# Delta rule with the heads in pairs: one generator for two heads, one inversion row for 64 blocks, shared buffer slots

## Chip, cores and metric

One core of one Trainium2 chip runs the whole program in one launch. The metric is the device time of the program in microseconds (us). The kernel before takes 1430.65 us, the median of 3 runs (1429.36 to 1430.66). Everything is fp32 at the program's edges; the large products are taken as sums of three products of "fp32r" halves (hi·hi, hi·lo, lo·hi).

## What is computed

One step of a decoder layer for a prompt of 1024 tokens and 8 samples of one token each, so 1032 columns in all. The normalised input is multiplied by one wide matrix `w_in`. Its columns feed a short gated convolution (branch A) and a gated DeltaNet with 8 heads of 128 by 128 (branch B); both are projected, gated, merged and projected again. What matters here is the delta rule of branch B, which runs in chunks (128 tokens in the kernel, so 8 chunks). In the reference, for one head and one chunk:

```python
decay = exp(where(causal, gc[:, None] - gc[None, :], -inf))
a_mat = where(strict, (kb @ k.T) * decay, 0) + eye(C)
u, w  = split(triangular_solve(a_mat, [v * beta, kb * exp(gc)]))
attn  = (q @ k.T) * decay
# scan over the chunks, state S (128 x 128):
v_new = u - w @ S
o     = (q * exp(gc)) @ S + attn @ v_new
S     = S * exp(gc_last) + (k * exp(gc_last - gc)).T @ v_new
```

q and k are l2-normalised, `gc` is the running sum of the log decay, and o then goes through an RMSNorm and a gate silu(zB). The 8 samples take one step each of the same recurrence from a given state, per head.

## The kernel before

Python generates a fixed instruction stream for the five engines. There are three stretches.

1. **Start** (`startup`): loads, norms, and the first product.
2. **Jobs** (`run`, line 708). A job is one 128-column slice of `w_in` against all 1032 columns of the input: 3 groups of 344 columns, 8 k-steps, 3 matmuls a step, so 72 matmuls. There are 48: per head a k, a q and a v job (`qkv_job`, line 829, whose evacuation copies PSUM to `raw` and whose follow-up generator does the 4-tap convolution and silu), 8 zB jobs (`zb_job`, line 1138) and 16 gate jobs (`gate_job`, line 1155, whose result is stored to DRAM). Each job's weights are loaded to `wraw` (`w_load`, line 688), and split into `whi` by ScalarE and `wlo` by VectorE (`w_split`, line 696) during the job before.
3. **Products** (`products`, `products_b`), then the output projections. These start from `to_products` (line 1700), which is hooked ahead of the third job from the end: it drains all generators, frees their buffers and starts to prepare operands.

Beside the jobs run generators ("strands"), one for each piece of side work: decays, delta rule, samples, convolutions. After every k-step of a job, `slot()` (line 602) resumes each strand whose own clock is due by the model in class `Sched` (line 62), which charges every instruction a cost and 450 ns of slack after each plain `yield`. So the order of the work on each engine follows a planner's costs, and a strand's TensorE work is put as a burst into a job, about between two of its k-steps.

For each head h there is a strand `decay_gen` (line 858: builds the 8 decay blocks DB and DA from a broadcast row of gc) and a strand `delta_gen` (line 886), which starts once v is there. Its steps, in order: transposes of k and q with squared sums (ScalarE) and kd (VectorE); rsqrt; the k·k and q·k products into DB and DA; the **row inversion** (line 984), 31 steps of two dependent VectorE instructions that invert all 32 by 32 diagonal blocks of the head's 8 chunks at once, 32 blocks on 128 partitions by 8 rows each, fetched through DRAM (sA, At before; sT, Tn after); then TensorE joins the 32-blocks to 64 and 128 ("inversion bursts" of 32 by 32 and 64 by 64 matmuls; lines 1015 to 1046); then the recurrence over 8 chunks, three bursts a chunk: k·S and q·S; U·X; kd·vn and DA·vn. VectorE makes X and S between them, ScalarE copies vn. Last, the norm, transposes and the product with sz, and a store to yBsc. Flags hold the heads in order: the inversion's result may enter U only when the head before is done (line 1006), and the buffers of head h wait for head h-2.

The sample work of head h is `sample_gen` (line 1231). It waits for the flag "qs", which `delta_gen` sets at its very beginning, and for the samples of the head before.

Buffers: `T4` is a set of 6 equal slots (class `Slots`, line 635) that are lent and given back; the strands' large tiles (U, DB, DA, kd, vp, kq) have buffers of their own, by two or three. `wraw` has two. The order of the jobs (lines 1383 to 1394) is k, q, v, one gate, then zB of the head before; eight more gates close it, with the last zB as the third of them.

On the DMA side, nearly all transfers are issued by SyncE, one queue in program order.

Of the kernel before, what the change touches and what calls it, by code (L numbers as in the profile page):

```python
# [16 lines left out]
P = 128  # L17
# [18 lines left out]
NT4 = 6  # L36
# [3 lines left out]
NSL, NSR = 22, 7  # L40
# [5 lines left out]
FILL = (1, 1, 1, 1, 1, 1, 1, 1)  # L46
# [15 lines left out]
class Sched:  # L62


    def __init__(self):
        self.clk = dict.fromkeys(("V", "A", "PE", "GP", "SY", "DMA"), 0.0)
        self.cur = None
        self.chain = True
        self.table = None
        self.cold, self.run = True, 0.0  # L70

    def note(self, eng, cost, lat=0.0):
# [42 lines left out]
class Paced:  # L115
# [3 lines left out]
    def __getattr__(self, op):  # L119
# [3 lines left out]
        def call(*args, **kw):  # L123
# [7 lines left out]
            elif n == "PE":  # L131
                if op == "transpose":
                    s.note(n, max(size, out.shape[0]) * 2 / 2.4 + 2.0)
                elif kw["rhs"].dtype == F32:
                    s.note(n, 4 * max(size, kw["lhsT"].shape[-1]) / 2.4 + 4.0)
# [22 lines left out]
def hybrid_step(  # L158
# [110 lines left out]
    gsc = dram.tile([NC * NH, C], F32, name="gsc")  # L269
# [9 lines left out]
    rsc = dram.tile([NH, NB, P], F32, name="rsc")  # L279

# [407 lines left out]
    def w_load(jobs, i):  # L688
# [3 lines left out]
        raw = wpool.tile([P, NK, P], F32, tag="wraw", name="wraw", bufs=2)  # L692
# [16 lines left out]
    def run(jobs, first, stop):  # L709
        for i in range(first, stop):  # L710
# [3 lines left out]
            if i + 2 < stop:  # L714
                w_load(jobs, i + 2)
            _, hi, lo = wq.pop(i)
            rh, rl = src()
            for gi, (g0, gn) in enumerate(GROUPS):
# [3 lines left out]
                for k in range(NK):  # L722
# [24 lines left out]
    def ba_gen():  # L747
        ap_ = bp
        ban = ap_.tile([P, 9, 16], F32, name="ban")
# [16 lines left out]
        xg = ap_.tile([P, 9, NH], F32, name="xg")  # L766
        u = ap_.tile([P, 9, NH], F32, name="u")
        sq = ap_.tile([P, 9, NH], F32, name="sq")
        pl = ap_.tile([P, 9, NH], F32, name="pl")
# [9 lines left out]
        for n in (17, 15, 13, 11, 9, 7, 5, 3):  # L779
# [22 lines left out]
        gcr = ap_.tile([64, C], F32, name="gcr")  # L802
        V.tensor_copy(out=gcr, in_=pt[:64, 0:C])
        SY.dma_start(out=gsc, in_=gcr)
# [4 lines left out]
                     in_=smp.rearrange("a b h -> (a b h)").unsqueeze(0).to_broadcast([P, 2 * NB * NH]))  # L809
        flags["ba"] = True  # L810
# [48 lines left out]
    def decay_gen(h, st):  # L859
        while not flags.get("ba") or (h and not flags.get(("qd", h - 1))) \  # L860
                or (h > 1 and not flags.get(("inv", h - 2))):
            yield
        gcB = bp.tile([P, NC, C], F32, tag="gcB", name="gcB")
        SY.dma_start(out=gcB, in_=gsc.rearrange("(c h) i -> h c i", h=NH)[h].unsqueeze(0).to_broadcast([P, NC, C]))
        yield
        while h > 1 and not flags.get(("done", h - 2)):
            yield
        DB = bp.tile([P, NC, C], F32, tag="DB", name="DB", bufs=2)
        DA = bp.tile([P, NC, C], F32, tag="DA", name="DA", bufs=2)
        for c in range(NC):  # L870
            act(DA[:, c, :], gcB[:, c, :], AF.Identity, bias=neg["gc"][:, c, h:h + 1])
            if c % 4 == 3:
                yield
        wide = lambda m: m.unsqueeze(1).to_broadcast([P, NC, C])
        tt(DB, DA, wide(m_strict), ALU.max)
        yield
        tt(DA, DA, wide(m_causal), ALU.min)
        yield
        act(DB, DB, AF.Exp, scale=-1.0)
        act(DA, DA, AF.Exp)  # L880
        act(gcB, gcB, AF.Exp)
        st.update(gcB=gcB, DB=DB, DA=DA)

    junk = lambda: bp.tile([P, C], F32, tag="junk", name="junk", bufs=1)

    def delta_gen(h, st):
        ch = lambda a: a[:, :, h:h + 1]
        while "DA" not in st or "v" not in st or (h > 1 and not flags.get(("done", h - 2))):
            yield
        kq, vT, gcB, DB, DA = st["kq"], st["v"], st["gcB"], st["DB"], st["DA"]  # L890
        V.tensor_copy(out=qs_s[:, h, :, 0], in_=smpl(kq[:, 0, :]))
        V.tensor_copy(out=qs_s[:, h, :, 1], in_=smpl(kq[:, 1, :]))
        V.tensor_copy(out=v_s[:, h, :], in_=smpl(vT))
        flags[("qs", h)] = True


        kd = bp.tile([P, NC, C], F32, tag="kd", name="kd", bufs=2)
        ssk = bp.tile([P, NC], F32, tag="ssk", name="ssk", bufs=2)
        ssq = bp.tile([P, NC], F32, tag="ssq", name="ssq", bufs=3)
        for src, sq in ((0, ssk), (1, ssq)):  # L900
            for half in range(2):
                pt = ps_aux()
                for i in range(4):
                    c = half * 4 + i
                    transpose(pt[:, i * C:(i + 1) * C], kq[:, src, c * C:(c + 1) * C])
                sched.loose()
                for i in range(4):
                    c = half * 4 + i
                    act(junk(), pt[:, i * C:(i + 1) * C], AF.Square, accum_out=sq[:, c:c + 1])
                if src == 0:  # L910
                    tt(kd[:, half * 4:half * 4 + 4, :], pt.rearrange("p (c d) -> p c d", d=C),
                       ch(ekd)[:, half * 4:half * 4 + 4, :].to_broadcast([P, 4, C]), ALU.mult)
# [4 lines left out]
        ts(ssk, ssk, EPS, op0=ALU.add)  # L917
        rk = rsqrt(bp, ssk, P, NC, "rk")
        cB = bp.tile([P, NC], F32, tag="cB", name="cB", bufs=2)
# [1010 lines left out]
```

## Time and profile before

The profiled execution took 1428.2 us, of which 1426.1 us lie between the first and the last instruction.

| stretch, us from the span's start | what runs | matmul busy, us | weight load busy, us | VectorE busy, us | ScalarE busy, us |
|---|---|---|---|---|---|
| 58 to 817 | jobs 1 to 47 and the delta rule | 748.64 | 718.28 | 520.03 | 432.07 |
| 817 to 1202 | products | 383.61 | 382.71 | 299.69 | 135.11 |
| 1202 to 1426 | end of the products, output projections | 215.57 | 190.88 | 129.37 | 65.95 |

A profile's matmul row counts overlapping, pipelined matmuls, and their ends are modelled; the weight loads (PEld) have a row of their own. An fp32 matmul shows as two matmul records, an fp32r one as one. The granted TensorE clock is 1.00 nearly everywhere in the span.

### The profile page before, as it was taken

To read this page: it belongs to the slowest core of one execution; us is meant where nothing else is said; L and a number is where in the kernel's file an instruction comes from. 1 tells how busy PE (TensorE), PEld (TensorE's weight loads), DVE (VectorE), ACT (ScalarE), POOL (GpSimd) and SP (SyncE) were. 2 spreads that over 40 slices of the span, in tenths; PEclk is the share of its full clock that TensorE was granted. 3 is DMA by queue.
4 is the path that set the end of the run, shared out by engine and by line. 5 is a ranking of instruction groups with operands and counts; after the bars stand their busy time and mean duration, and the time that the engine had idled before them with its cause. 6 is when DMAs were issued, how large, how long until landed. Compare 5 with 4: busy or idle time off the path is not lost.

```text
span 1426.1 us, 26358 instructions
## 1 busy us (share of the span) xinstructions
PE 1394.4 (98%) x10274; PEld 1328.4 (93%) x10274; DVE 990.5 (69%) x2516; ACT 674.7 (47%) x1534; POOL 31.0 (2%) x72
## 2 busy tenths in 40 slices
PE   6999999999999999999999999999999999999997
PEld 4899998999989899998999999999999999999786
DVE  6766875697758768676463988877777787854553
ACT  6756744856466555747433433333333345432211
POOL 0000000000000000000000000000000110000000
PEclk9999999999999999999899999999999999999999
DMA  9622432153412423241332465432211876752321
GB/s 321 145 48 78 118 97 72 33 125 82 108 55 70 121 51 104 68 108 56 96 104 73 133 224 178 134 90 75 61 54 59 231 225 213 239 161 86 96 85 60
DMA packets 191591, 161.80 MB, mean 113 GB/s; under 512 B 34503, under 2 KB 167008, under 8 KB 191458
## 3 DMA queue, kind: packets, MB, share of 16 engines
q1 hardware_dynamic: 186912, 151.58, 36.0%
q0 software_dynamic: 4352, 8.46, 2.1%
q8 instruction: 81, 1.33, 0.4%
q14 instruction: 44, 0.36, 0.1%
q10 hardware_dynamic: 202, 0.08, 0.0%
HBM read 123.40 MB, written 36.91 MB: 112 GB/s over the span
## 4 chain that ended last, share of the span: by engine, by line
PE 78%; DVE 10%; DMA 6%; ACT 3%; issue 2%; SPq 1%; DVEq 0%; ACTq 0%
PE pm_t L124 53%; PE pa_t L124 23%; PE pb L124 2%; DVE wlo L124 1%; DVE Ttmp L124 1%; DVE Tw L124 1%; DMA At<-sA 1%; DVE acc L124 1%; SPq L124 1%; DMA xs<-in_x_prompt_dram 1%; DMA gcB<-gsc 1%; DVE on L124 1%; DVE mrg L124 1%; DVE vT L124 1%; DVE ro_a L124 0%
## 5 line engine op out<-in xcount | busy, mean ns | idle before, releaser
L124 PE MATMUL pm_t<-xh,whi 128*128 128x344 f32 (+1 forms) x1384 | 453.4, 328 | 0.0
L124 PE MATMUL pm_t<-xl,whi 128*128 128x344 f32 (+1 forms) x1384 | 436.2, 315 | 0.0
L124 PE MATMUL pm_t<-xh,wlo 128*128 128x344 f32 (+1 forms) x1384 | 435.8, 315 | 0.0
L124 PEld LDWEIGHTS pm_t<-xh,whi 128*128 128x128 f32 x1384 | 261.6, 189 | 1.6
L124 PEld LDWEIGHTS pm_t<-xl,whi 128*128 128x128 f32 x1384 | 261.8, 189 | 0.4
L124 PEld LDWEIGHTS pm_t<-xh,wlo 128*128 128x128 f32 x1384 | 261.2, 189 | 0.4
L124 ACT CAST whi<-wr 128x1024 fp32r<-128x1024 f32 x60 | 62.8, 1047 | 139.4 <-PE pm_t L124 65.7
L124 DVE TENSOR_TENSOR wlo<-wraw,whi 128x512 fp32r<-128x512 f32 x112 | 76.5, 688 | 35.6 <-ACT whi L124 35.1
L124 ACT CAST whi<-wraw 128x512 fp32r<-128x512 f32 x112 | 68.7, 624 | 55.8 <-PE pm_t L124 53.0
L124 PE MATMUL pm_t<-thi,wlo 128*128 128x258 f32 x304 | 86.3, 284 | 1.3 <-DVE wlo L124 1.2
L124 PE MATMUL pa_t<-thi,wlo 128*128 128x258 f32 x304 | 86.2, 284 | 0.1
L124 PE MATMUL pm_t<-tlo,whi 128*128 128x258 f32 x304 | 85.9, 283 | 0.0
L124 PE MATMUL pa_t<-tlo,whi 128*128 128x258 f32 x304 | 85.9, 283 | 0.0
L124 PE MATMUL pm_t<-thi,whi 128*128 128x258 f32 x304 | 85.8, 282 | 0.0
L124 PE MATMUL pa_t<-thi,whi 128*128 128x258 f32 x304 | 85.8, 282 | 0.0
L124 DVE TENSOR_TENSOR wlo<-wr,whi 128x1024 fp32r<-128x1024 f32 x60 | 73.2, 1220 | 10.3 <-ACT whi L124 10.1
L124 PE MATMUL pa_t<-xh,whi 128*128 128x258 f32 x256 | 72.4, 283 | 0.0
L124 PE MATMUL pa_t<-xh,wlo 128*128 128x258 f32 x256 | 72.2, 282 | 0.0
L124 PE MATMUL pa_t<-xl,whi 128*128 128x258 f32 x256 | 72.2, 282 | 0.0
L124 DVE SCALAR_TENSOR_TENSOR kq<-raw,vecs,kq 128x528 f32<-128x528 f32 x96 | 69.6, 761 | 2.4 <-ACT kq L124 2.4
L124 PE MATMUL pm_t<-ylo,whi 128*128 128x344 f32 x192 | 61.4, 321 | 0.6 <-DVE ylo L124 0.6
L124 PE MATMUL pm_t<-yhi,whi 128*128 128x344 f32 x192 | 61.4, 321 | 0.0
(397 smaller groups left out, 3065.5 us busy)
## 6 DMA issues: line engine op xcount, KB each, us to landing
wraw<-in_w_in_dram SPq DMA_DIRECT2D x48, 512.0 KB
wr<-in_w_in_dram SPq DMA_DIRECT2D x64, 256.0 KB
aw<-in_ada_w_dram SPq DMA_DIRECT2D x16, 512.0 KB
gBsc<-gate SPq DMA_DIRECT2D x8, 516.0 KB
gAsc<-gate SPq DMA_DIRECT2D x8, 516.0 KB
txs<-phi SPq DMA_DIRECT2D x8, 516.0 KB
txs<-plo SPq DMA_DIRECT2D x8, 516.0 KB
yAsc<-acc SPq DMA_DIRECT2D x8, 516.0 KB
```

The source lines that it names most:

```text
L124: r = f(*args, **kw)
```

## The change

- `delta_gen(p)` and `decay_gen(p)` serve a **pair** of heads, p = 0 to 3. Every TensorE burst holds the matmuls of both heads; small tiles (ssk, cB, nx, vs) have a head axis; VectorE's X and S steps are two instructions in a row, ScalarE's vn copy is one of twice the width.
- The **row inversion** is one for 64 blocks: 16 rows on each partition instead of 8, still 31 steps of two instructions. The 32-block joins take 4 bursts for a pair.
- The delta strand starts after the pair's last q job; v is asked for only after the inversion, and the "qs" flag, on which the samples wait, is set there. kd is parked in DRAM (kdsc) and fetched back. The decay exp(gc) of q comes as a row of its own from DRAM; DA and DB are each built from gc (four broadcast loads a pair).
- **Slots**: T4 has 16 slots of 1032 columns; U, T11, kd, DA, DB, sz, and later wlo and wsum live there. `wraw` has one buffer, and the next load is issued after the split that frees it.
- **Job order**: k q k q v v g g for pair 0; k q, zB of the pair before twice, k q v v g g for pairs 1 and 2; the last pair has four gates and its own two zB jobs; six gates close.
- **Planner**: a cost for TensorE's change between fp32 and fp32r work; the 4 us pause in `sample_gen` is gone.

Core of the diff:

```diff
-NT4 = 6
+WRAW = 1
+NT4 = 16
 DYN = 2048
 HT = NT // 2
 PW = HT // 2
-NSL, NSR = 22, 7
+NSL, NSR = 14, 7
 SAME = 115.0
 CROSS = 60.0
 LATER = {"PE": 200.0, "V": 135.0, "A": 155.0}
 SLK = 450.0
 SG = 0
-FILL = (1, 1, 1, 1, 1, 1, 1, 1)
+ORDER = (
+    "k0 q0 k1 q1 v0 v1 g g",
+    "k0 q0 y0 y1 k1 q1 v0 v1 g g",
+    "k0 q0 y0 y1 k1 q1 v0 v1 g g",
+    "k0 q0 y0 y1 k1 q1 v0 v1 g g g g z0 z1",
+)
...
+        if eng == "PE" and wide != self.wide:
+            cost += 85.0 if self.wide else 20.0
+            self.wide = wide
...
             if before:
                 before()
-            if i + 2 < stop:
-                w_load(jobs, i + 2)
...
                     if gi == 1 and k in (1, 4) and i + 1 < stop:
                         w_split(jobs, i + 1, k == 4)
+                        if k == 4 and i + 2 < stop:
+                            w_load(jobs, i + 2)
...
+        def decays(dst, i, mask, op, scale):
+            while not T4.ready(2):
+                yield
+            g_ = T4.get("gcB", S)
+            gcB = g_.rearrange("p (c i) -> p c i", i=C)
+            SY.dma_start(out=gcB, in_=gsc[0].rearrange("(c h) i -> h c i", h=NH)[h0 + i].unsqueeze(0)
+                         .to_broadcast([P, NC, C]))
+            yield
+            for c in range(NC):
+                act(dst[:, c, :], gcB[:, c, :], AF.Identity, bias=neg["gc"][:, c, h0 + i:h0 + i + 1])
+                if c % 4 == 3:
+                    yield
+            T4.give(g_)
+            tt(dst, dst, wide(mask), op)
+            yield
+            act(dst, dst, AF.Exp, scale=scale)
+            yield
+
...
+        while p and not flags.get(("got", p - 1)):
+            yield
...
         for j in range(31, 0, -1):
-            r0 = j // 4
-            n = 8 - r0
+            r0 = j // 2
+            n = 16 - r0
             tv = tmp[:, 0:n * j].rearrange("p (n w) -> p n w", w=j)
-            tt(tv, Tw[:, r0:8, j:j + 1].to_broadcast([P, n, j]),
+            tt(tv, Tw[:, r0:16, j:j + 1].to_broadcast([P, n, j]),
                At[:, j:j + 1, 0:j].to_broadcast([P, n, j]), ALU.mult)
-            tt(Tw[:, r0:8, 0:j], Tw[:, r0:8, 0:j], tv, ALU.add)
+            tt(Tw[:, r0:16, 0:j], Tw[:, r0:16, 0:j], tv, ALU.add)
             yield 0.0
         T4.give(At_)
-        for g in range(4):
-            sched.loose(g < 3)
-            SY.dma_start(out=sT[h, :, :, g::4, :].rearrange("c b r j -> (c b) r j"), in_=Tw[32 * g:32 * g + 32])
-        Tn = bp.tile([P, NC, 32], F32, tag="Tn", name="Tn")
-        Un = bp.tile([P, NC, 32], F32, tag="Un", name="Un")
-        SY.dma_start(out=Tn, in_=sT[h].rearrange("c b r j -> (b r) c j"))
-        yield
-        while h and not flags.get(("done", h - 1)):
-            yield
-        V.transpose(out=Un.rearrange("p c j -> p (c j)"), in_=Tn.rearrange("p c j -> p (c j)"))
-        Qs = bp.tile([P, NC, 64], F32, tag="Qs", name="Qs")
+        for g in range(2):
+            sched.loose(g < 1)
+            SY.dma_start(out=sT[hp, :, :, g::2, :].rearrange("h c b r j -> (h c b) r j"), in_=Tw[64 * g:64 * g + 64])
...
+        while p and not flags.get(("done", p - 1)):
+            yield
+        while not T4.ready(5):
+            yield
+        kd_ = [T4.get("kd", S) for _ in range(2)]
...
+        flags[("got", p)] = True
+        sched.loose()
+        for i in range(2):
+            GP.memset(U[i][64:128, :, 0:64], 0.0)
+            GP.memset(U[i][32:64, :, 0:32], 0.0)
+            GP.memset(U[i][96:128, :, 64:96], 0.0)
+        GP.memset(T11[0:32, :, 32:64], 0.0)
...
+        for n in range(2):
+            b1, b2 = blk(n)
+            for c in range(W):
+                PE.matmul(pt[b1, c, :], lhsT=DB[c // NC][b2, c % NC, b1], rhs=Un[b2, c, :], start=True, stop=True)
+        for n in range(2):
+            A.copy(out=Qs[blk(n)[0], :, 0:32], in_=pt[blk(n)[0]])
+        yield
+        pt, pt2 = (ps_aux().rearrange("p (c j) -> p c j", j=32) for _ in range(2))
...
+        while "v1" not in st:
+            yield
+        v = st["v"]
+        vp = v[:, :, 0:S].rearrange("p h (c d) -> p h c d", d=C)
+        V.tensor_copy(out=v_s[:, hp, :], in_=v[:, :, S + 3:S + 32:4])
+        flags[("qs", p)] = True
...
+                pk = bank()
+                for i in range(2):
+                    PE.matmul(pk[:, i], lhsT=kq[:, i, 0, cs], rhs=Sp[:, i], start=True, stop=True)
+                X = vp[:, :, c, :]
+                for i in range(2):
+                    stt(X[:, i], pk[:, i], nx[:, i, c:c + 1], X[:, i], ALU.mult, ALU.add)
+                yield
+            pv = bank()
+            for i in range(2):
+                PE.matmul(pv[:, i], lhsT=U[i][:, c, :], rhs=X[:, i], start=True, stop=True)
+            vn = two("vn")
+            A.copy(out=vn, in_=pv)
+            yield
+            pS, po = bank(), bank()
+            for i in range(2):
+                PE.matmul(pS[:, i], lhsT=kd[i][:, c, :], rhs=vn[:, i], start=True, stop=True)
+            t_pe = sched.cur.t
+            for i in range(2):
+                if c:
+                    PE.matmul(po[:, i], lhsT=kq[:, i, 1, cs], rhs=Sp[:, i], start=True, stop=False)
+                PE.matmul(po[:, i], lhsT=DA[i][:, c, :], rhs=vn[:, i], start=c == 0, stop=True)
+            t_po, sched.cur.t = sched.cur.t, t_pe
+            Sn = two("S")
             if c == 0:
-                po = ps_aux()
-            PE.matmul(po[:, 0:C], lhsT=DA[:, c, :], rhs=vn, start=c == 0, stop=True)
-            Sn = bp.tile([P, C], F32, tag="S", name="S", bufs=2)
-            if c == 0:
-                V.tensor_copy(out=Sn, in_=pS[:, 0:C])
+                V.tensor_copy(out=Sn, in_=pS)
             else:
-                stt(Sn, Sp, egl[:, c, h:h + 1], pS[:, 0:C], ALU.mult, ALU.add)
+                for i in range(2):
+                    stt(Sn[:, i], Sp[:, i], egl[:, c, h0 + i:h0 + i + 1], pS[:, i], ALU.mult, ALU.add)
             Sp = Sn
             sched.loose()
-            A.copy(out=on[:, c, :], in_=po[:, 0:C])
-            act(junk(), po[:, 0:C], AF.Square, accum_out=so[:, c:c + 1])
-            yield
-        store(n_delta_p[0, 0, h], Sp)
-        flags[("done", h)] = True
+            t_pe, sched.cur.t = sched.cur.t, t_po
+            A.copy(out=vp[:, :, c, :], in_=po)
+            for i in range(2):
+                act(junk(), po[:, i], AF.Square, accum_out=so[:, i, c:c + 1])
+            sched.cur.t = t_pe
+            sched.loose(False)
+            yield
...
-        sched.cur.t += 4000.0
-        yield
+        yield
+        while not T4.ready():
+            yield
+        rB_ = T4.get("rB", S)
...
-    for h in range(NH):
+    for p in range(NH // 2):
         i0 = len(jobs)
-        stz.append(head_jobs(h))
-        if h:
-            hook(i0, lambda h=h: start(sample_gen(h - 1)))
-        for _ in range(FILL[h]):
-            gate_job(*gates.pop(0))
-        if h:
-            zb_job(h - 1, stz[h - 1])
+        pair_jobs(p)
+        if p:
+            hook(i0, lambda p=p: (start(sample_gen(2 * p - 2)), start(sample_gen(2 * p - 1))))
     iga = len(jobs)
-    for n, g in enumerate(gates):
+    for g in gates:
         gate_job(*g)
-        if n == 1:
-            zb_job(NH - 1, stz[NH - 1])
...
-            v = raw[src] if src else sums.pop(g)
+            yield from when(lambda: T4.ready())
+            lo_ = T4.get("wlo", D)
+            hi, lo = hi_.rearrange("p k c -> p (k c)"), lo_.bitcast(F32R)
```

More of the change, by code (lines that the diff above doesn't have):

```diff
@@ L70, in __init__, with note @@
         self.cold, self.run = True, 0.0
-    def note(self, eng, cost, lat=0.0):
+        self.wide = False
+    def note(self, eng, cost, lat=0.0, wide=False):
         if self.cur:
@@ new lines, in delta_gen @@
+        for n in (1, 0):
+            b1, b2 = blk(n)
+            for i in range(2):
+                A.copy(out=U[i][b1, :, b2], in_=pt[b1, NC * i:NC * i + NC])
+        sched.loose()
+        A.copy(out=T11[32:64, :, 0:32], in_=pt2[32:64])
+        sched.loose(False)
+        yield
+        pts = [ps_aux().rearrange("p (c j) -> p c j", j=64) for _ in range(2)]
+        for c in range(W):
+            PE.matmul(pts[c // NC][0:64, c % NC, :], lhsT=DB[c // NC][64:128, c % NC, 0:64], rhs=U[c // NC][64:128, c % NC, 64:128],
+                      start=True, stop=True)
@@ new lines, in delta_gen @@
+        for i in range(2):
+            A.copy(out=Qs[0:64, NC * i:NC * i + NC], in_=pts[i][0:64])
+        for d in st["db"]:
+            T4.give(d)
+        flags[("inv", p)] = True
+        yield
+        pts = [ps_aux().rearrange("p (c j) -> p c j", j=64) for _ in range(2)]
+        for c in range(W):
+            PE.matmul(pts[c // NC][0:64, c % NC, :], lhsT=T11[:, c, :], rhs=Qs[0:64, c, :], start=True, stop=True)
+        for i in range(2):
+            A.copy(out=U[i][0:64, :, 64:128], in_=pts[i][0:64])
@@ new lines, in delta_gen, with pair_jobs, kqdst, dst @@
+            sched.join("V")
+            store(yBsc[h, :, 0:S], v[:, i, 0:S])
+            T4.give(sz)
+        flags[("out", p)] = True
+    def pair_jobs(p):
+        st = {}
+        def kqdst(i, j):
+            def dst():
+                if i + j == 0:
+                    st["kq"] = bp.tile([P, 2, 2, CY], F32, tag="kq", name="kq", bufs=2)
+                return st["kq"][:, i, j, :]
+            return dst
+        def vdst(i):
+            def dst():
+                if i == 0:
+                    st["v"] = bp.tile([P, 2, CY], F32, tag="v", name="v")
+                return st["v"][:, i, :]
+            return dst
+        def post(key, then=None):
+            def f(d):
+                st[key] = True
+                if then:
+                    start(then(p, st))
+            return f
+        def gate():
+            if gates:
+                gate_job(*gates.pop(0))
+        first = lambda: p < 2 or flags.get(("done", p - 2))
+        def job(c):
+            kind, i = c[0], int(c[1]) if c[1:] else 0
+            h = 2 * p + i
+            if kind == "k":
+                qkv_job(COL_K + h * P, 8 + h, (lambda: "kq" in st) if i else first, kqdst(i, 0),
+                        post(f"k{i}", None if i else decay_gen))
+            elif kind == "q":
+                qkv_job(COL_Q + h * P, h, lambda: "kq" in st, kqdst(i, 1), post(f"q{i}", delta_gen if i else None))
+            elif kind == "v":
+                qkv_job(COL_V + h * P, 16 + h, lambda: not p or flags.get(("out", p - 1)), vdst(i), post(f"v{i}"))
+            elif kind == "z":
+                zb_job(h)
+            elif kind == "y":
+                zb_job(h - 2)
+            else:
+                gate()
+        for c in ORDER[p].split():
+            job(c)
```

427 lines of the change are left out of this document (208 added, 219 removed).

## The prediction, made before the changed kernel was run

> **What bounds the kernel now.** I read the page first, then the windows by stretch, then the waits of TensorE's weight loads in the stretch that the change touches, then single bursts in the timeline.
>
> ```profile
> span 1426.1 us, 26358 instructions
> PE 1394.4 (98%) x10274; PEld 1328.4 (93%) x10274; DVE 990.5 (69%) x2516; ACT 674.7 (47%) x1534; POOL 31.0 (2%) x72
> 58.00:817.00 759.00, 748.64 (x5601) 718.28 (x5600) 520.03 (x1671) 432.07 (x1183) 16.20 (x42) 0.99 0.32 86
> 817.00:1202.00 385.00, 383.61 (x3192) 382.71 (x3191) 299.69 (x473) 135.11 (x189) 11.59 (x16) 1.00 0.45 138
> ```
>
> TensorE is the bound: 98% of the span. In the stretch of the jobs, 58 to 817 us, matmuls are idle for 759.00 - 748.64 = 10.4 us, but that row counts overlapping matmuls with modelled ends; weight loads are idle for 759.00 - 718.28 = 40.7 us. No matmul is removed by the change: two heads need the same products alone or in step. So what it can win lies between these two numbers: the losses between matmuls. Their list, weight loads first, matmuls behind:
>
> ```profile
> PEld pa_t L124 <- issue: 7.0, 32, 0.4
> PEld pa_t L124 <- DVE X L124: 6.7, 18, 1.6
> PEld pa_t L124 <- ACT vn L124: 4.9, 21, 0.9
> PEld pa_t L124 <- DVE on L124: 4.5, 9, 0.9
> PEld pa_t L124 <- DVE S L124: 3.6, 14, 0.7
> PEld pa_t L124 <- DVE kd L124: 2.2, 2, 1.8
> ...
> PEld pa_t L124 <- ACT Qs L124: 1.1, 3, 0.7
> PEld pa_t L124 <- DVE Un L124: 0.7, 1, 0.7
> PEld pa_t L124 <- ACT T L124: 0.7, 3, 0.2
> PE pa_t L124 <- DVE X L124: 2.5, 4, 1.3
> ...
> PE pa_t L124 <- ACT vn L124: 1.2, 2, 0.6
> ...
> PE pa_t L124 <- DVE S L124: 0.8, 2, 0.4
> ```
>
> Each row is total us, times, longest. X, vn and S are the three bursts of a recurrence step: 15.2 us together, 53 waits of 0.29 us. The rest hang on the inversion (issue, Qs, Un, T) and on each head's ends (on, kd). DVE and ACT have 239 and 327 us free in the stretch, so they matter only through such waits.
>
> **The change part by part.**
>
> *Inversion bursts.* Before, 32 bursts show the "issue" idle. One of them:
>
> ```profile
> 749.57 0.31 PE L124 MATMUL pm_t<-xh,wlo 128*128 128x344 f32 x1
> 749.82 1.14 PE L124 MATMUL pa_t<-U,DB 64*64 64x64 f32 x16
> 750.89 0.43 PE L124 MATMUL pm_t<-xh,whi 128*128 128x344 f32 x1
> 751.15 0.32 PE L124 MATMUL pm_t<-xl,whi 128*128 128x344 f32 x1
> 751.31 0.32 PE L124 MATMUL pm_t<-xh,wlo 128*128 128x344 f32 x1
> ```
>
> Main matmuls start 0.16 us apart (751.15, 751.31). From 749.57 to 751.15 are 1.58 us for two of them (0.32) and 16 small ones at about 0.06 (the next rows' first and last start, 749.8 and 750.7): 0.96. So 0.30 us goes to the change to a burst and back. The pair needs 4 bursts (4 pairs: 16) where 32 were: 16 x 0.30 = **-4.8 us**. The small matmuls' number stays.
>
> ```profile
> L124 PE MATMUL pa_t<-U,DB x16: 218/218/267, 749.8 to 750.7; 64*64 64x64 f32 x16
> ```
>
> *Recurrence steps.* 23 bursts a head become 23 a pair. If a burst waits as often and as long, half of 15.2 goes: -7.6 us; by the matmul rows (4.5) it is -2.2. Against it, a step is longer:
>
> ```profile
> L124 DVE SCALAR_TENSOR_TENSOR X<-pa_t,nx,vp 128x128 f32<-128x128 f32 x56 | 19.5, 348 | 20.2 <-PE pa_t L124 20.2
> L124 DVE SCALAR_TENSOR_TENSOR S<-S,egl,pa_t 128x128 f32<-128x128 f32 x56 | 19.3, 344 | 36.1 <-PE pa_t L124 35.9
> ```
>
> X and S are now two instructions in a row, 0.35 us more each. If each of the 92 waiting bursts waited its 0.29 us with no gain from halving, that would be 26.7 us, +11.5. But the planner charges both instructions, so I take **-5**, near to the halving; ends -7.6 and +11.5. The Qs, Un and T waits (2.5 us) halve: **-1.2**. on and kd stay, since each head still has its own: 0.
>
> *Row inversion.* 496 VectorE instructions become 248, each with twice the rows:
>
> ```profile
> L124 DVE TENSOR_TENSOR Ttmp<-Tw,At 128x76 f32<-128x76 f32 x8 | 1.9, 237 | 0.3
> L124 DVE TENSOR_TENSOR Ttmp<-Tw,At 128x8 f32<-128x8 f32 x8 | 1.3, 166 | 0.2
> ```
>
> 68 more elements cost 71 ns, 1.04 ns each. The sizes (8 - j//4)·j have a mean of 50, the new (16 - j//2)·j of 92: about 210 becomes 254 ns. 496 x 0.210 = 104 us becomes 63: 41 us of VectorE freed, on an engine that is 69% busy. It is covered by TensorE already, so 0 by itself; only a shorter queue ahead of X and S could turn it into time (a rival). ScalarE's 64 more bias steps and the kd round trip, q rows and further gc rows by DMA (32 transfers of 512 KB, some 17 MB on 86 GB/s x 759 us = 65 MB, at a DMA share of 0.32) lie beside TensorE: 0. If a stall comes of them, it is DVE's queue waiting in order behind such a row, with w_split and the convolutions behind it.
>
> *One wraw buffer.* The load now starts after the split that frees it, and SyncE waits there, with the delta strand's sA, At, sT and Tn transfers queued behind. It has from group 1, step 4 of a job to group 1, step 1 of the next, 21 steps of 3 x 0.16 = 10 us.
>
> ```profile
> 91.25 8.89 DMA gcB<-gsc
> ```
>
> The longest 512 KB transfer on the chain of work takes 8.9 us, so 10 just covers it. I take **+1**; ends 0 and +5 (a quarter of 44 loads late by half a microsecond).
>
> *Start and tail.* Pair 0 starts later, but TensorE has jobs then: 0. The end is tighter. Head 7 alone:
>
> ```profile
> L124 PE MATMUL pa_t<-ident,kq x16: 271/272/273, 661.0 to 669.9; 128*128 128x128 f32 x16
> L124 DVE SCALAR_TENSOR_TENSOR DB<-pa_t,cB,DB x8: 340/341/351, 693.3 to 699.0; 128x128 f32<-128x128 f32 x8
> L124 DVE TENSOR_TENSOR Ttmp<-Tw,At x31: 156/211/236, 714.9 to 734.1; 128x60 f32<-128x60 f32 x3, 128x28 f32<-128x28 f32 x2, 128x54 f32<-128x54 f32 x2, 128x48 f32<-128x48 f32 x2
> L124 ACT COPY on<-pa_t x8: 265/266/267, 755.3 to 781.9; 128x128 f32<-128x128 f32 x8
> L124 SPq DMA_DIRECT2D yBsc<-on x1: 319/319/319, 788.2 to 788.2; - x1
> L124 ACT COPY gate<-pm_t x18: 438/445/449, 735.7 to 816.4; 128x344 f32<-128x344 f32 x18
> ```
>
> From its transposes to its store are 127 us, and the last gate is evacuated 28 us later. A pair adds 16 squares with their sums (16 x 0.48, rows below), a second set of products (some 6 us, as 693 to 699), 62 x 0.044 in the inversion, 8 steps x 0.8, and a second output (4): 27, so 154 us. Now also the samples wait: "qs" comes only after the inversion, about 50 us ahead of the pair's end, and one sample took 36 us from its first matmul to its last state:
>
> ```profile
> L124 ACT ACTIVATE junk<-pa_t 128x128 f32<-128x128 f32 x192 | 53.7, 280 | 3.6 <-PE pa_t L124 1.6
> L124 ACT ACTIVATION_READ_ACCUMULATOR junk<-pa_t 128x1 f32 x192 | 38.7, 202 | 0.2
> L124 PE MATMUL pa_t<-sm_prod,ones x2: 186/228/269, 670.6 to 670.7; 128*128 128x24 f32 x2
> L124 DVE SCALAR_TENSOR_TENSOR S<-S,sm_egs,rB x8: 340/344/347, 700.4 to 705.3; 128x128 f32<-128x128 f32 x8
> ```
>
> Less the removed 4 us pause, two in a row end at 154 - 50 + 2 x 32 = 168 us, plus the final norm, 172. From the last q job to the draining point lie 11 jobs, 11 x 72 x 0.16 = 127 us, and the pair's own TensorE work: 759 us less 47 jobs (541) over four pairs, 54. That is 181 against 172 and 8 for q's convolution: it just fits. I take **+1**; ends 0 and +15.
>
> *Slots.* In its inversion a pair holds 2 each of DA, DB, kd and U, with T11, Tn/Un and Qs 11 of the 16; the next pair's DA, two sz and a sample's state make 16. A gate or zB evacuation that finds none waits, and its PSUM bank and the main matmuls behind it. No row shows such a wait for T4 before; at worst a pair waits 1 us, +4. I take 0, since the inversion's slots come back within some 10 us and four PSUM banks stand between. The products, with wlo and wsum in slots, have 30 slots for what used 28 and its own buffers, about one fewer: 0, since TensorE never waits there now (382.71 us of weight loads in 385, the second window above).
>
> *Sum*: -4.8 - 5 - 1.2 + 1 + 1 = -9.0 us. The profiled execution is 1428.2 us (span and 2.1 around it): 1419.2. The median of the runs is 2.45 above it: **1421.6**.
>
> **The rivals.**
>
> *Half clock at the larger bursts* (slower). Once before, TensorE lost its clock:
>
> ```profile
> 676.90:680.30 3.40, 3.40 (x50) 3.29 (x48) 0.52 (x4) 2.71 (x11) 0.00 (x0) 1.00 0.03 7
> 677.87 1.84 PE L124 MATMUL pa_t<-qs_s,S 128*128 128x2 f32 x16
> 680.30:690.50 10.20, 10.20 (x64) 8.58 (x63) 3.17 (x8) 3.32 (x6) 0.00 (x0) 0.50 0.22 55
> ```
>
> Ahead of it were 3.4 us of tiny matmuls (32 by 32, and two columns), and it cost half of 10.2, 5.1 us. The change makes 64 to 96 tiny matmuls one burst. It decides if such a burst leaves too few wide matmuls in a few microseconds; once in each pair is 4 x 5.1 less the 5.1 that is there, +15.3: 1436.9. Against it: the heads' own inversions ran at full clock, seven of eight. The Trainium skill, TensorE: Matmul & The Clock Gate, section "Part 1: The HAM clock gate", says that the clock is halved after an idle window of about 3.4 us and that activity releases it; by that rule no burst would trip it, and this rival's price is 0. The trace disagrees, with 3.40 of 3.40 us busy just before.
>
> *Late tail* (slower). The last two samples end some 12 us after the draining point, the products' operands are late by that, and TensorE waits for them: 1421.6 + 12 = 1433.6. For it: three estimates added. Against: three jobs (34 us) still follow.
>
> *No gain* (same). The longer steps wait as much as two short ones; only the inversion's -4.8 is left, and load and tail take 2 to 3 of it: 1428.5. It is also what comes if the planner's order splits the pair's bursts again.
>
> *More* (faster). VectorE's freed 41 us empty the queue: X, vn, S, Qs, Un and T waits all go (17.7), on too (4.5), with 4.8 that is -27: 1403.7.
>
> **How the numbers follow.** Forecast 0.52, half clock 0.14, late tail 0.11, no gain 0.13, more 0.10. Faster than 0.2% (2.9 us, about what a measurement of this kernel can tell from no change): 0.52 + 0.10 = 0.62; same 0.13; slower 0.14 + 0.11 = 0.25. The forecast's own range has the recurrence between -7.6 (load and tail at 0: 1417) and +2 (1428.6). For 8 in 10 it runs to 1405, most of the way to "more", and to 1437, the half clock.
>
> **What would show it.** Right: matmul records unchanged in number; "issue" waits at about 16; X, vn and S waits of weight loads near 8 us; the last gate evacuated by about 808 us; Ttmp rows x124 at some 254 ns. Wrong: clock 0.50 beside the pairs' inversions; an idle TensorE between the last pair's samples and the products; SyncE or ScalarE waiting for wraw; X and S waits as before or longer.

## The result, and the profile after

The changed kernel takes 1490.1 us (median of 4 runs, 1487.5 to 1491.9) where the kernel before takes 1430.0 (4 runs, 1427.9 to 1430.7): ratio 1.042, 95% interval 1.040 to 1.044. It is slower by 60 us; the forecast was 1421.6 and faster.

The page of the changed kernel, the lines that answer to those of before, and the packets of its transfers (191591 before, 167008 of them under 2 KB):

```profile
span 1490.2 us, 26003 instructions
PE 1411.7 (95%) x10274; PEld 1360.0 (91%) x10274; DVE 946.1 (63%) x2140; ACT 664.7 (45%) x1501; POOL 46.2 (3%) x97
DMA packets 209205, 176.49 MB, mean 118 GB/s; under 512 B 34135, under 2 KB 183088, under 8 KB 209074
```

The matmul records are as many as before, and VectorE's busy time fell by 44 us, as reckoned. But TensorE fell from 98% to 95% of a longer span. The windows by stretch show where (columns: stretch, its length, busy time of TensorE's matmuls, its weight loads, VectorE, ScalarE and GpSimd, granted clock, DMA share, GB/s):

```profile
58.00:880.00 822.00, 769.82 (x5622) 752.76 (x5621) 474.32 (x1295) 419.23 (x1148) 31.42 (x67) 0.94 0.38 99
880.00:1264.00 384.00, 379.62 (x3155) 378.37 (x3154) 297.57 (x468) 136.00 (x190) 11.59 (x16) 1.00 0.44 135
1264.00:1490.00 226.00, 217.20 (x1213) 193.17 (x1211) 132.73 (x273) 67.89 (x102) 0.00 (x0) 0.99 0.38 129
```

The products and what follows take 384 and 226 us, where they took 385 and 224. The stretch of the jobs takes 822 instead of 759. Two things happened in it: weight loads are idle for 69 us (41 before), and the mean clock is 0.94 (0.99 before), which is 0.06 x 822 = 49 us of lost clock, a part of it in time that was idle anyway. Who ends the idle time of the weight loads, and then the longest of the matmuls (total us, times, longest):

```profile
PEld pa_t L134 <- issue: 22.4, 15, 8.1
PEld pa_t L134 <- DVE TU L134: 9.0, 3, 4.3
PEld pa_t L134 <- ACT U L134: 7.8, 2, 5.0
PEld pa_t L134 <- ACT vn L134: 7.1, 9, 3.4
PEld pm_t L134 <- ACT raw L134: 6.9, 1, 6.9
PEld pa_t L134 <- DVE kdp L134: 5.1, 4, 4.2
```

```profile
PE pa_t L134 <- DVE v L134: 16.2, 4, 7.8
```

Before, no wait of TensorE in this stretch was longer than 1.8 us. Now there are nine of 3 to 8 us in the matmuls' row, all behind VectorE or ScalarE. What these two waited for themselves:

```profile
ACT DA L134 <- DMA gcB<-gsc: 45.1, 8, 12.1
...
DVE kq L134 <- DMA eg<-gsc: 32.3, 7, 8.2
...
ACT whi L134 <- DMA wraw<-in_w_in_dram: 27.9, 6, 8.6
...
ACT DB L134 <- DMA gcB<-gsc: 25.5, 6, 7.4
```

That is 103 us of waits for broadcast rows (gcB and eg), where the kernel before had 4.6:

```profile
ACT DA L124 <- DMA gcB<-gsc: 4.6, 2, 3.8
```

One case in the timelines of SyncE, VectorE and TensorE, with the idle time ahead of an instruction and its releaser in brackets:

```profile
332.11 0.99 SPq L134 DMA_DIRECT2D eg<-gsc  x2
...
341.19 1.23 DVE L134 TENSOR_TENSOR kq<-kq,eg 128x1024 f32<-128x1024 f32 x1 [6.66 <-DMA eg<-gsc]
345.97 1.23 DVE L134 TENSOR_TENSOR kq<-kq,eg 128x1024 f32<-128x1024 f32 x1 [3.04 <-DMA eg<-gsc]
...
350.60 1.73 PE L134 MATMUL pa_t<-ident,v 128*128 128x128 f32 x7 [7.82 <-DVE v L134]
```

SyncE issues two eg rows at 332 us. By the cost in its model, the planner thinks that such a row takes some 3.3 us and puts its reader into VectorE's queue accordingly; the rows land 9 and 13 us after their issue. VectorE takes its instructions in order, so the norm of the pair's output, which stands in the tile v by then and on which its transposes wait, comes behind the rows, and TensorE runs dry for 7.8 us.

### The profile page after: what moved, and what is told of

It reads as the page before. It is cut to its first block, busy times and chain, and to the rows that moved or that the text cites. A ratio compares the mean times of both kernels' runs of the same rounds, so it can differ in the third digit from the quotient of the medians.

```text
span 1490.2 us, 26003 instructions
## 1 busy us (share of the span) xinstructions
PE 1411.7 (95%) x10274; PEld 1360.0 (91%) x10274; DVE 946.1 (63%) x2140; ACT 664.7 (45%) x1501; POOL 46.2 (3%) x97
## 3 DMA queue, kind: packets, MB, share of 16 engines
q1 hardware_dynamic: 204528, 166.29, 38.6%
## 4 chain that ended last, share of the span: by engine, by line
PE 68%; DMA 15%; DVE 8%; ACT 6%; issue 2%; SPq 1%; POOL 0%; DVEq 0%; ACTq 0%
PE pm_t L134 44%; PE pa_t L134 22%; DMA gcB<-gsc 7%; DMA eg<-gsc 2%; PE pb L134 2%; SPq L134 1%; DVE wlo L134 1%; DVE Ttmp L134 1%; DVE Tw L134 1%; ACT DA L134 1%; ACT junk L134 1%; DVE acc L134 1%; ACT L134 1%; DMA At<-sA 1%; DMA TU<-sT 1%
## 5 line engine op out<-in xcount | busy, mean ns | idle before, releaser
L134 PE MATMUL pm_t<-xh,wlo 128*128 128x344 f32 (+1 forms) x1384 | 443.1, 320 | 0.0
L134 PE MATMUL pm_t<-xl,whi 128*128 128x344 f32 (+1 forms) x1384 | 442.9, 320 | 0.0
L134 PEld LDWEIGHTS pm_t<-xh,whi 128*128 128x128 f32 x1384 | 269.1, 194 | 7.8 <-ACT raw L134 6.9
L134 PEld LDWEIGHTS pm_t<-xl,whi 128*128 128x128 f32 x1384 | 269.1, 194 | 0.0
L134 PEld LDWEIGHTS pm_t<-xh,wlo 128*128 128x128 f32 x1384 | 268.1, 194 | 0.2
L134 DVE TENSOR_TENSOR acc<-pm_t,acc 128x258 f32<-128x258 f32 x112 | 45.2, 422 | 25.6 <-PE pm_t L134 25.4
L134 PE MATMUL pm_t<-yhi,wlo 128*128 128x344 f32 x192 | 61.4, 320 | 0.0
```

The source lines that it names most:

```text
L134: r = f(*args, **kw)
```

## The experiments

Theory 1 was that: rows that land late, in front of engines that wait in order. Theory 2 was the rival of the prediction: the pair's bursts of small matmuls lose the clock, which shows as windows with a granted clock of 0.50. Theory 3 was the single wraw buffer. A fourth came up on the way. Each time is the median of 4 to 10 runs, each ratio is to the kernel before, with its 95% interval.

### Four edits, one for each theory

Planning the readers later (theory 1), `rows_later`:

```diff
             SY.dma_start(out=gcB, in_=gsc[0]...)
+            sched.cur.t += 7000.0
             yield
```

The same line stands behind the eg loads.

> The changed kernel, in which the planner counts 7 us more for each of the 16 gcB loads and 8 eg loads (512 KB broadcast rows), so that what reads them is put into the engines' queues 7 us later. Nothing is computed otherwise. Theory 1 (ScalarE and VectorE are put in front of a row that has not landed, TensorE runs dry behind them and then loses its clock): the eight stalls of TensorE that end at pa_t<-ident,kq, ident,v, vn,kd and at ACT raw, 42 us together, and the half clock behind them, some 48 us of windows or 24 us of time, go for the most part: 1430 to 1442 us; ACT and DVE wait under 20 us for gcB and eg, where they wait 103 now. Theory 2 (the pair's bursts of small matmuls lose the clock, the rows are waited for beside it): the windows at 0.50 stay at 12 or more of 15, and of the 47 us that they cost no more than 10 come back; with the idle stalls gone 1450 to 1465. Theory 3 (the single wraw buffer): ACT still waits for wraw and TensorE for ACT, 1480 to 1490.

1487.2 us, ratio 1.041 (1.038 to 1.043). Theory 1 had it at 1430 to 1442, so in this form it failed: ScalarE and VectorE still waited 85 us for rows, and the stalls came back at other places, the longest of 17.9 us. The readers came later and some of the rows as well (the first eg row is issued at 192.7 us instead of 168.0).

Two weight buffers (theory 3):

```diff
-WRAW = 1
-NT4 = 16
+WRAW = 2
+NT4 = 15
...
             w_ap, c0, n, src, before, evac, after = jobs[i]
...
+            if i + 2 < stop:
+                w_load(jobs, i + 2)
...
-                        if k == 4 and i + 2 < stop:
-                            w_load(jobs, i + 2)
```

> The changed kernel with two wraw buffers, the load issued at the start of a job as in the kernel before, and 15 slots instead of 16 to pay for it. Theory 1 (rows): wraw is waited for only since its load is queued behind rows; 28 us of ScalarE's waits for wraw go, but one TensorE stall alone (7.1 us at raw) hangs on them: 1478 to 1492. Theory 2 (bursts): no change, 1485 to 1495. Theory 3 (single buffer): the loss of 60 us goes for the most part: 1430 to 1450.

1450.4 us, 1.015 (1.012 to 1.018): 40 us of the 60 come back. Only theory 3 had come near that, though 66 us of waits for rows were left.

Smaller bursts (theory 2): each of the four joins is split by head, `for i in range(2): ... yield`.

> The changed kernel with the pair's four bursts of joining matmuls cut into eight, one per head and step, with the planner's pause between; the same matmuls. Theory 1 in its strict form (only idle loses the clock): 16 more bursts of 0.30 us, 1490 to 1497, and the windows at 0.50 at 247, 414 to 431, 602 and 773 us stay. Theory 2 (bursts lose the clock): these windows, 34 us or 17 us of time, go, so 1475 to 1481; if bursts explain all windows at 0.50, 1445 to 1455. Theory 3: 1490 to 1497.

1477.4 us, 1.033 (1.031 to 1.036): 13 us back, as theory 2 had it (1475 to 1481), and the windows at 0.50 behind the pairs' bursts are gone but for one, at 265 us.

The kernel before, its row loaded late (theory 1 the other way round): the gcB load of `decay_gen` is moved below the wait for head h-2.

> The kernel before, with one edit: each head's gcB load is issued where its reader is about to be planned (behind the wait for head h-2) instead of well ahead of it. Nothing of the pairs is in it. Theory 1 (rows read too early): ScalarE waits some 5 us at each of 8 rows (8.9 us to land, 3.3 planned and 0.45 slack), 30 to 45 us in all where it waits 4.6 now; TensorE stalls at a part of them and loses its clock after those longer than 3.4 us: 1440 to 1475. Theory 2 and theory 3: 1428 to 1433, since bursts and buffers are those of before.

1428.6 us, 0.999 (0.998 to 1.001). This says nothing: the trace shows the eight loads issued at the same times as before (91.0 to 618.6 us; before 91.3 to 608.5). SyncE runs ahead, and it seems that the buffer, not the place in the program, set the time of the load.

### Two buffers, taken further

The single buffer in the kernel before: every second wraw buffer is taken by a tile that nobody uses, and the load is issued after the split, as in the change.

> The kernel before with the change's wraw rule alone in the jobs: one buffer, the load issued after the split that frees it. Theory 3 in its plain form (10 us of lead are too short for the load, whatever else runs): the 40 us that two buffers gave back in the pairs kernel are lost here too, 1455 to 1475. Theory 3 joined with theory 1 (the single buffer ties SyncE's queue to VectorE's split, and costs where the broadcast rows and the strands' transfers behind it are read soon after they are planned): the kernel before reads 8 rows and not 24, well after their load, so 1430 to 1442.

1428.5 us, 0.999 (0.998 to 1.001): theory 3 in its plain form is wrong. Ten us of lead were enough there, with 8 rows on the queue and not 24.

Both edits of above in the changed kernel, two buffers and small bursts:

> The changed kernel with two wraw buffers and the joins cut per head, both edits of the runs before. If the two losses are separate, their gains add: 1450.4 less 13 is 1437, range 1433 to 1443, and no window at 0.50 starts in a burst of joining matmuls. If the bursts only lost the clock because the engines were late, the cut gives nothing more and costs 16 times 0.30 us: 1450 to 1456.

1483.6 us, 1.037 (1.034 to 1.041). The gains of 40 and 13 don't add; together they are 6.5. Each edit of this kind gives the planner another order: if the 10274 matmuls of each trace are listed in order, by tiles and shapes, the four edits of the changed kernel so far differ from it in 1172 to 1634 lines. Stalls of 11 to 12 us turned up elsewhere, ScalarE up to 12.0 us ahead of a gcB row among what caused them. A fourth theory offered itself: the order decides, and these numbers are luck. Against it spoke the two edits of the kernel before, which moved 1954 and 1594 lines and no time.

### The rows in one piece

gc and exp(gc) lie in DRAM as rows of one chunk and one head, so a broadcast row of a head is eight pieces of 512 bytes for each of 128 partitions. The next edit stores them head by head; a partition then reads one piece of 4 KB. Same values, same bytes.

```diff
-        SY.dma_start(out=gsc[0], in_=gcr)
+        for c in range(NC):
+            SY.dma_start(out=gsc[0].rearrange("(h c) i -> c h i", c=NC)[c], in_=gcr[c * NH:c * NH + NH])
...
-            SY.dma_start(out=gcB, in_=gsc[0].rearrange("(c h) i -> h c i", h=NH)[h0 + i]...)
+            SY.dma_start(out=gcB, in_=gsc[0].rearrange("(h c) i -> h c i", h=NH)[h0 + i]...)
```

> As the run before, and gc and its exponential are stored head by head in DRAM, so that a partition of a broadcast row is one run of 4 KB and not eight of 512 bytes; same values, same sizes. If the many small pieces make the rows land late (theory 1), they land in well under 9 us, the waits of ScalarE and VectorE for gcB and eg fall from some 65 us to under 30, and the time to 1422 to 1433. If a row lands late since it stands behind others in the queue, within 4 us of the run before.

On top of two buffers and small bursts: 1426.6 us, 1.000 (0.998 to 1.002), 57 us less than without. But the planner counted eight stores for one, and 296 lines of TensorE's order moved. Its opposite was run beside it, rows in pieces and the readers of rows and TU planned later:

> As two buffers and small bursts, and the planner counts 7 us more for each gcB and eg row and 3.5 us more for the fetch of the inverted blocks (TU). Theory 1: with the single buffer's tie gone the planner's later order now holds on the chip, the waits for rows fall to some 20 us and the two or three stalls at pa_t<-TU,DB go: 1420 to 1432. If later planning only moves the waits elsewhere, as it did with one buffer (1487 against 1490), within 4 us of the run without it.

1484.1 us, 1.039 (1.036 to 1.042): planning later doesn't help with two buffers either.

To hold the order still, the planner is now told of one store of the whole size, and the eight are issued past it. Now 16 to 22 lines differ on TensorE from the kernel with the same edits and rows in pieces (the first expectation below has 229 and 4800 by another listing of the same work). The four combinations:

> The changed kernel; gc and exp(gc) stand head by head in DRAM (stored in eight parts each, which the planner counts as the one store of before), so that each partition of a gcB or eg row is read as one piece of 4 KB. The planner's order is the changed kernel's: on TensorE 229 lines of 8472 differ, not 4800 as with the edits of the planner. Theory 1 (rows land too late for engines that wait in order): rows land in 6 to 7 us instead of 9 to 12, the waits of ScalarE and VectorE for gcB and eg fall from 103 to under 35 us, and the time to 1425 to 1445. Theory 3 (single wraw buffer): ScalarE's 28 us of waits for wraw stay, 1475 to 1490. A fourth theory, that the order of the work as such decides (each edit of the planner gave another order, and two buffers gave 40 us alone and lost them again with the small bursts): the order is kept, so 1480 to 1495.

> The run with two wraw buffers (1450.4) with the rows in one piece and the planner's order kept. Theory 1: the waits for rows fall from 66 to under 25 us, 1420 to 1432. Theory 3: two buffers were the gain, 1445 to 1455. Fourth theory (order): 1445 to 1455.

> The run with the joins cut per head (1477.4) with the rows in one piece and the order kept. Theory 1: 1420 to 1435. Theory 3 and fourth theory: 1470 to 1482. With the run of one piece alone beside it: whether the large bursts cost their 17 us at half clock with the rows out of the way (theory 2), or nothing.

> The run with two buffers and small bursts (1483.6) with the rows in one piece and the order kept; the run at 1426.6 had the same three edits, but the planner counted eight stores there and made another order. Theory 1: 1420 to 1435 again. Fourth theory (the 57 us were the order's): 1470 to 1485.

| edits to the changed kernel | rows in pieces of 512 bytes, us | rows in one piece of 4 KB, us | ratio to before, 95% interval |
|---|---|---|---|
| none | 1490.1 | 1418.0 | 0.993 (0.991 to 0.996) |
| two wraw buffers | 1450.4 | 1403.3 | 0.983 (0.981 to 0.986) |
| small bursts | 1477.4 | 1416.5 | 0.993 (0.990 to 0.995) |
| both | 1483.6 | 1421.2 | 0.995 (0.993 to 0.998) |

The piece size gives 47 to 72 us in each line, at nearly the same order. The fourth theory is out as the cause of the loss, and theory 1 is right in its core: it is the rows, and what they need to land. One row of pair 3 in the chain of waits, in the changed kernel, then with the rows in one piece:

```profile
607.85 9.09 DMA gcB<-gsc
```

```profile
549.81 4.55 DMA gcB<-gsc
```

The waits for rows with one piece: 13.6 us where 103 were, and the wait for wraw goes with them (0.9 us where 27.9 were), although the buffer is still a single one:

```profile
ACT DB L134 <- DMA gcB<-gsc: 5.6, 3, 2.0
DVE kq L134 <- DMA eg<-gsc: 5.4, 5, 1.7
...
ACT DA L134 <- DMA gcB<-gsc: 2.6, 4, 0.8
...
ACT whi L134 <- DMA wraw<-in_w_in_dram: 0.9, 2, 0.7
```

The version with two buffers beats both kernels, by 27 us (1.7%) the one before; its jobs (58 to 787 us) ran at full clock:

```profile
58.00:787.00 729.00, 726.08 (x5588) 711.76 (x5587) 466.96 (x1290) 419.01 (x1145) 33.78 (x65) 1.00 0.38 110
```

### Is it the wait for the row, or what the pieces do to others?

The kernel before with its rows in one piece:

> The kernel before with gc head by head in DRAM, so that its 8 gcB rows are read as pieces of 4 KB. Theory 1: it reads its rows well after their load (ScalarE waits 4.6 us for gcB in all, TensorE for none of it), so 1424 to 1431; the gain of rows in one piece belongs to the pairs kernel, which reads 24 rows at once. If the pieces cost by what they do to all other transfers, the kernel before gains about a third of the 72 us, 1400 to 1412.

1424.1 us, 0.996 (0.993 to 0.998), at the edge of what theory 1 had: some 6 us, not a third of 72. The kernel before has little to gain from better rows, the pairs kernel much.

The pairs kernel with rows in one piece, and 24 row loads in pieces, from DRAM to DRAM, which nobody reads (the first run below); the same with the spare loads in one piece; and the first with two wraw buffers:

```diff
+        nc.sync.dma_start(out=spare[nsp[0]], in_=gs8[k].rearrange("(c h) i -> h c i", h=NH)[h].unsqueeze(0).to_broadcast([P, NC, C]))
```

> The pairs kernel with rows in one piece (1418.0), and behind each of the 24 row loads the same row once more in 128 times eight pieces of 512 bytes, from DRAM to a part of DRAM that nobody reads: the small pieces are there, but no engine waits for them. Theory 1a (only the wait for the row itself costs): 1415 to 1428. Theory 1b (the small pieces hold the DMA engines, and all transfers behind them, weights and the inversion's blocks, land late): 1450 to 1490, with waits for wraw, At and TU.

> As the run with 24 spare row loads that nobody reads (1486.3; they were all issued between 93 and 224 us, since nothing holds them back), with the spare loads in one piece of 4 KB a row part: the same bytes from and to the same places, the same order on TensorE, VectorE, ScalarE and GpSimd. If the number of pieces is what holds the DMA engines: 1415 to 1435. If the bytes do (12.6 MB in 130 us), 1470 to 1490.

> The pairs kernel with rows in one piece and two wraw buffers (1403.3) and the 24 spare loads in small pieces. In the run with one wraw buffer ScalarE waited 64 us for weights. If the single buffer is what turns slow transfers into a TensorE stall, the second buffer takes a good part: 1415 to 1450, wraw waits under 30 us. If the rows and the inversion's blocks stall it as much, 1460 to 1475.

1486.3 us with spare pieces (1.039, 1.035 to 1.044), 1420.7 with spare loads in one piece (0.994, 0.990 to 0.997), 1465.8 with spare pieces and two buffers (1.025, 1.022 to 1.028). Nothing holds the spare loads back, so all 24 were issued between 93 and 224 us (162 in one piece). That stretch, first with pieces, then in one piece; the order on TensorE, VectorE, ScalarE and GpSimd is the same in the two:

```profile
93.00:224.00 131.00, 90.81 (x560) 88.73 (x558) 42.34 (x75) 61.88 (x168) 5.15 (x7) 0.87 0.69 151
```

```profile
93.00:224.00 131.00, 131.00 (x856) 130.66 (x855) 86.16 (x189) 90.61 (x226) 10.20 (x17) 1.00 0.67 208
```

With pieces the DMA engines are as busy (0.69 and 0.67) for fewer bytes (151 and 208 GB/s), and TensorE stands still for 40 of the 131 us. So it is the rows' layout in pieces, not their bytes, and the pieces cost without being waited on: what lands late is everything behind them. In the run with pieces that was the weights first of all:

```profile
ACT whi L134 <- DMA wraw<-in_w_in_dram: 64.1, 9, 21.4
```

With the second buffer this wait is 5.8 us, but the spare pieces still cost 62.5 us there (1465.8 against 1403.3), where they cost 68 with one buffer (1486.3 against 1418.0): other transfers are late too (one wait of ScalarE, 31.8 us, ended at a gate's store, one of VectorE, 31.5 us, at eg).

```profile
ACT DA L134 <- DMA gBsc<-gate: 31.8, 1, 31.8
DVE kq L134 <- DMA eg<-gsc: 31.5, 1, 31.5
...
ACT whi L134 <- DMA wraw<-in_w_in_dram: 5.8, 1, 5.8
```

So a single buffer is not what makes late transfers dear. The spare loads came within 131 us, the rows of the changed kernel over some 600; how much of its 72 us comes from waits for the rows themselves, and how much from what they delay, the runs do not tell apart.

### The half clock

Rows in one piece, two buffers (1403.3 us, clock 1.00), and 32 of a pair's matmuls of T and Q issued three times over:

```diff
+                for _ in range(2):
+                    nc.tensor.matmul(pt[b1, c, :], lhsT=Tn[b1, c, :], rhs=Qs[b1, c, 0:32], start=True, stop=True)
                 PE.matmul(pt[b1, c, :], lhsT=Tn[b1, c, :], rhs=Qs[b1, c, 0:32], start=True, stop=True)
```

> The pairs kernel with rows in one piece and two wraw buffers (1403.3, clock 1.00 throughout), in which 32 of the 96 small matmul records groups of the second join, T times Q, are issued three times over, with the same result: 64 more 32 by 32 matmuls (128 records, 3.8 us at 30 ns) a pair, without a pause, 15.4 us in all. If the clock halves after a window of 3.41 us in which the array is idle, it stays at 1.00: 1403.3 plus 15.4, 1416 to 1422. If it halves after a window in which the array does little, however busy TensorE is (in the runs so far each such window held less than some 2750 columns over all 128 rows, where a window of main matmuls holds 6900), each pair's burst of some 6.8 us holds one such window whole: four or more windows at 0.50 right behind the bursts, each 3.4 us or longer, 1424 to 1438.

1431.7 us, 28.4 more: 15.4 for the added matmuls, as reckoned above, and the remaining 13 beside 37.4 us of windows at 0.50 (at half the clock these can cost at most half of that, 18.7). Two of the four bursts, each the window before the fall and what follows:

```profile
231.70:235.10 3.40, 3.40 (x116) 3.40 (x113) 3.02 (x5) 0.76 (x1) 0.00 (x0) 1.00 0.52 134
235.10:241.90 6.80, 6.80 (x71) 6.74 (x68) 1.75 (x4) 2.92 (x6) 0.21 (x1) 0.50 0.31 90
...
709.60:713.00 3.40, 3.40 (x117) 3.40 (x114) 0.00 (x0) 0.15 (x1) 0.00 (x0) 1.00 0.62 161
713.00:723.20 10.20, 10.20 (x125) 9.55 (x123) 0.00 (x0) 2.41 (x6) 0.00 (x0) 0.50 0.02 5
```

All four pairs lost the clock behind their burst, with matmuls and weight loads busy for the whole window. An idle array is not needed.

## Why the prediction was wrong, point by point

- **The failed step** is "ScalarE's 64 more bias steps and the kd round trip, q rows and further gc rows by DMA (32 transfers of 512 KB, some 17 MB on 86 GB/s x 759 us = 65 MB, at a DMA share of 0.32) lie beside TensorE: 0." It counted bytes. 16 of the 32 are broadcast rows in 1024 pieces each; with the 8 that were there before the changed kernel loads 24. Put in one piece, these 24 give 72 us back, the whole loss and 12 us more. The warning stood in a row that the prediction quoted, 8.89 us for one gcB row: 512 KB in that time are 59 GB/s, with the DMA engines 0.32 busy on the mean. It was used only as a measure for a weight load. The next sentence named the stall that came, VectorE's queue "waiting in order behind such a row", but gave it no price and no chance.
- **One wraw buffer, +1, ends 0 and +5.** By itself 0, as the kernel before with one buffer shows. In the changed kernel ScalarE waited 27.9 us for wraw, and without the pieces 0.9: the bound took the longest load of the trace of before, and the change itself made loads longer. What two buffers give is not settled: -40 and +6 us with rows in pieces, -15 and +5 in one piece (without and with small bursts each time). Since the order of the work moves with the edit each time, the runs don't say which part is the buffer's.
- **Half clock at the larger bursts, 14%, +15.3.** The mechanism was right and it came: of 15 falls of the clock in the jobs four followed a window that TensorE had filled with small matmuls (those at 247.3, 421.4, 602.3 and 773.0 us, 30.7 us at 0.50, so at most 15.4 us of time), the other eleven one in which it stood idle in part. Small bursts gave 13 us back, in another order of the work. But it was not what made the kernel slower; with the rows in one piece the small bursts give 1.5 us, within the error. Two windows of the changed kernel and what follows each, once behind a burst and once behind an idle stretch:

```profile
243.90:247.30 3.40, 3.40 (x95) 3.19 (x95) 2.70 (x4) 1.86 (x4) 0.00 (x0) 1.00 0.35 74
247.30:250.70 3.40, 3.40 (x22) 3.34 (x20) 2.16 (x4) 1.33 (x4) 0.20 (x1) 0.51 0.30 85
...
370.20:373.60 3.40, 0.00 (x0) 0.00 (x0) 3.40 (x6) 0.00 (x0) 0.00 (x0) 1.00 0.98 142
373.60:380.40 6.80, 3.91 (x14) 3.91 (x15) 5.81 (x14) 6.71 (x15) 4.57 (x2) 0.50 0.70 220
```

  The second pair is also the rows' doing at its plainest: DMA 98% busy at 142 GB/s, and TensorE with nothing to do. By the rule of the Trainium skill, TensorE: Matmul & The Clock Gate, "Part 1: The HAM clock gate", an idle window halves the clock; the second pair agrees; in the first the window was busy, and the clock fell all the same.
- **The other terms** hold roughly once the rows are out of the way. The forecast was 1421.6, and the kernel with rows in one piece takes 1418.0; that they lie so near is partly luck, since rows in one piece gave the kernel before 6 us as well, and the terms below miss on both sides. Its waits of the weight loads in the jobs:

```profile
PEld pm_t L134 <- ACT raw L134: 3.9, 1, 3.9
PEld pa_t L134 <- issue: 3.3, 14, 0.4
PEld pa_t L134 <- ACT vn L134: 2.5, 7, 0.8
PEld pa_t L134 <- DVE v L134: 2.3, 3, 1.6
PEld pa_t L134 <- DVE kdp L134: 1.5, 4, 0.6
```

  14 "issue" waits (about 16 were forecast), 3.7 us less than the 7.0 of before (4.8 were forecast). The waits for vn and for v, the tile that holds the recurrence's X, are 4.8 us together, and there is none for S, where 15.2 were: -10 instead of -5. The row inversion's Ttmp is x124 at 255 ns (254 were forecast). The last gate is evacuated at 799.2 us (808 were forecast; 877.7 in the changed kernel), so there is no late tail. Slots: 0, no wait in the list points at one.
- **What the pairs are worth** with rows alike: 1418.0 against 1424.1 us for the kernel before with rows in one piece. The two intervals overlap, so the 6 us are likely and not shown; with two buffers it is 21 us, and that is shown.

## What to carry to other kernels

A transfer is priced by its pieces and by what stands behind it on the queue, not by its bytes: before adding loads of a kind, divide the bytes of one in the trace by its time, and if the rate is low, ask why. An engine that takes its work in order turns a late row into a stall of TensorE, and planning the reader later doesn't help while the queue itself is late. Where each edit reorders the whole program, hold the order still and change one thing in memory instead; only then did four runs agree.

## What the runs showed of the hardware

- 512 KB broadcast to 128 partitions took 9.1 us in pieces of 512 bytes and 4.6 in pieces of 4 KB (the two rows above, each beside other transfers). By the pages of the profile, the packets of the queue took 38.6% of 1490.2 us with the rows in pieces and 38.3% of 1416.2 us without, 575 and 542 us on all 16 engines: an estimate of 33 us more for the 24 rows, less than half of what TensorE lost. The Trainium skill, DMA: Bandwidth & Descriptors, "Specifications", gives 512 bytes as the least transfer for full rate; no run here supports that: DMA engines that were 0.69 busy in the run with the spare pieces of 512 bytes moved 151 GB/s, and 0.67 busy with spare pieces of 4 KB they moved 208. Whether the size of a piece does it or that the eight lie 4 KB apart was not tried. The 48 weight loads of the jobs come in pieces of 512 bytes too (128 columns of 4 bytes in each row of `w_in`), in every kernel here, and no run changed that.
- The clock is decided in windows of 3.41 us on a fixed grid: the falls at 247.3 and 773.0 us of the changed kernel lie 525.7 us apart, 154 times 3.413, and each stay at 0.50 is a multiple (3.4, 6.8, 10.2, 13.65). The Trainium skill, TensorE: Matmul & The Clock Gate, "Part 1: The HAM clock gate", gives a window of 3413 ns that runs freely, and the traces agree.
- It falls after a window in which the array does little, busy or not. Counted from the matmul records of all runs between 80 and 840 us, as columns times rows in use over 128: all 95 falls followed a window with at most 2752, and no window at full clock under 1568 was without a fall; the median window without a fall holds 6500 to 7200. Between 1568 and 2752 both came. The pairs' bursts, uncut, did not always trip it: with two buffers and rows in one piece none of the four did, with one buffer two. That this hangs on where a burst lies on the grid would follow from such a count, but was not tried by itself.
